# Building the expert gate table in two halves of 64 tiles instead of one table of 128

## The chip, the cores and the metric

One core of one Trainium2 chip runs the whole program in one launch. The metric is the device time of one execution in microseconds (us), median over runs.

## The reference

A two-layer decoder trunk over 256 tokens with a model width of 1024. Layer 0 mixes by a short gated convolution, layer 1 by attention; behind each stands the same expert mixer, and only that one is touched here. For each token it picks, per head, 16 of 128 x 128 experts, and sums gate x gelu(x . u) x v over them:

```python
q = (xc @ w_q).reshape(PEER_CHUNK, PEER_HEADS, 2, PEER_HALF)
s1 = einsum('thd,nd->thn', q[:, :, 0], sub_k1); s2 = einsum('thd,nd->thn', q[:, :, 1], sub_k2)
v1, i1 = top_k(s1, 16); v2, i2 = top_k(s2, 16)
cand = v1[..., :, None] + v2[..., None, :]
cidx = i1[..., :, None] * 128 + i2[..., None, :]
top_s, top_pos = top_k(cand, 16)
e_idx = take_along_axis(cidx, top_pos); g = softmax(top_s)
a = gelu(einsum('td,thkd->thk', xc, u_emb[e_idx]))
out = einsum('thk,thkd->td', g * a, v_emb[e_idx])
```

## The kernel before, in words

The kernel computes the mixer densely. All 16384 experts are gone through as 128 **tiles** of 128 experts; a tile is one item of a list that every stage takes its weights from (`items`, line 93). `A` holds, for 128 experts (partitions), 128 tiles and 256 tokens, first gelu(x . u), and after multiplication by the gate table the weight of each expert for each token. An expert's number is 128 x e1 + e2, where e1 is the tile and e2 the partition.

**Getting an item ready.** Weights arrive by DMA into one of three `RAW` buffers (`issue`, line 126). A u tile is turned by VectorE into `TR` (line 153). ScalarE rounds the item to a reduced 4-byte format as `HI` (line 164), and the difference goes into `LO` (line 168): on GpSimd, in two pieces of 128x512, for u tiles; on VectorE, in one piece of 128x1024, for v tiles. Each kind of buffer exists three times. `next_item` (line 213) prepares items n+1 to n+3, issues the products of item n and then lets `run_side` issue side work.

**u tiles** (`u_mm`, line 885). 24 products of 128x256: 16 with HI (lines 748, 749) and 8 with LO (line 752), into one half of a PSUM bank of the lower four (`lo4`). After each odd tile `out_pair` applies Gelu to the pair.

**v tiles** (line 988). 12 products of 128x512 (line 453), with `A` as the stationary operand, accumulate the output in the upper four banks (`hi4`). Every four tiles `wsplit` (lines 962, 963) splits the next four slices of `A` on ScalarE and VectorE.

**Side work.** A queue of operations with a price each; every item brings a budget (1.62 for u tiles, 1.25 for v tiles), and an operation is issued when the budget covers it. During the first u tiles this is the top-k search. After it, `listed` (line 831) turns the lists of e1, e2 and gate to the tokens, and `g_side` (line 895) builds the gate table, 8 tokens at a time, 32 groups per layer:

- `hots` (line 909): one VectorE comparison of 128x2048 makes the one-hot rows of e1 and e2 for 8 tokens;
- `gated` (line 918), twice: a VectorE product of 128x1024 puts the gate, in two parts, into the one-hot of e1, for 4 tokens each;
- its matmuls (line 925): 8 for each `gated`, 128 x 128 stationary, 128 columns moving, into `hi4`; issued on TensorE after a later u tile's products;
- `copied` (line 935): for tiles whose Gelu is still to come, ScalarE copies the table into `A`;
- `mult` (line 942): for tiles whose Gelu is done, VectorE multiplies `A` by the table.

A pair whose Gelu comes when part of the table already lies in `A` is multiplied by it afterwards, in `out_pair` (lines 864, 868 and 872). All of the table is built beside the u tiles: `u_last` empties the side queue before the first v tile.

Of the kernel before, what the change touches and what calls it, by code (L numbers as in the profile page):

```python
# [35 lines left out]
def trunk_kernel(ctx: ExitStack, tc, x, norm_mix, norm_ffn, conv_w_in, conv_w, conv_w_out,  # L36
# [26 lines left out]
    iota_t = sb.tile([128, 128, 2], F16, name="iota_t")  # L63
    OH = xbuf.bitcast(F16).rearrange("p (a b k t) -> p a b k t", a=5, b=TOK // 2, t=2)
    OH2 = (OH[:, 0], OH[:, 2])
    OH1 = OH[:, 1]
    ohg2 = sb.tile([128, 2, TOK // 4, 128, 2], F16, name="ohg2")
    OHG = [OH[:, 3 + i].rearrange("p (a b) k t -> p a b k t", a=2) for i in range(2)] + [ohg2]
    eT = sb.tile([128, T // TOK, 2, TOK // 2, 2], F16, name="eT")
    gT2 = sb.tile([128, T // 4, 2, 2, 2], F16, name="gT2")  # L70
# [211 lines left out]
    def late_consts():  # L282
        cwr = scratch(16384, 128)
        sp.dma_start(cwr[0:24], conv_w[0].rearrange("k (c p) -> (k c) p", p=128))
        pool.iota(iota_t, pattern=[[1, 128], [0, 2]], base=0, channel_multiplier=0,
                  allow_small_or_imprecise_dtypes=True)
# [407 lines left out]
    def peer(l):  # L694
# [27 lines left out]
        U0 = Q0 + H  # L722
        on_pool.update(range(Q0, U0))
# [119 lines left out]
        gates = lists[2].rearrange("p (s b t) -> p s b t", b=2, t=2)
# [5 lines left out]
        st = {"tiles": 0, "toks": 0, "prod": deque(), "multed": 0, "copied": deque(), "late": None, "listed": False}  # L849

        def late():

            f, st["late"] = st["late"], None
            if f:
                f()

        def out_pair(j, bk):

            late()
            assert 2 * j + 2 <= 95 or st["listed"]  # L860
            k, n = 2 * j, st["toks"]
            v = bk.rearrange("p (k t) -> p k t", t=256)
            if n:
                act.activation(v[:, :, 0:n], v[:, :, 0:n], AF.Gelu)

                def f():
                    w = A[:, k:k + 2, 0:n]
                    dve.scalar_tensor_tensor(w, v[:, :, 0:n], 1.0 / GSC, w, op0=OP.mult, op1=OP.mult)  # L868
                st["late"] = f
                credit[0] -= 0.1 + 0.0021 * n  # L870
            if n < T:
                act.activation(A[:, k:k + 2, n:T], v[:, :, n:T], AF.Gelu)  # L872
            st["tiles"] = k + 2

        def prod(before=NI, last=2 * T):

            while st["prod"]:
                n, q, f = st["prod"][0]
                if n > before or q > last or q // 2 > st["multed"] + 1:
                    return  # L880
                st["prod"].popleft()
                f()
                credit[0] += 0.45

        def u_mm(k):
            def f(hi, lo):
# [3 lines left out]
                if k % 2:  # L890
                    out_pair(k // 2, bk)
# [3 lines left out]
        def g_side():  # L895

            NG = T // TOK

            def tk(s, k0, k1):
                return psum[:, 2048 + s % 2 * 1024:3072 + s % 2 * 1024].rearrange(  # L900
                    "p (t k) -> p k t", k=128)[:, k0:k1]

            def spread(v):

                return v.rearrange("p a b t -> p (a b) t")[:, :, None, :].to_broadcast([128, TOK, 128, 2])

            def hots(s):
                a = s % 2
                dve.tensor_tensor(OH[:, a:a + 2].rearrange("p a b k t -> p (a b) k t"),  # L909
                                  iota_t[:, None].to_broadcast([128, TOK, 128, 2]), spread(eT[:, s]), op=OP.is_equal)  # L910

            def gated(q):

                s, h = q // 2, q % 2
                prod(last=q - 3)
                assert len(st["prod"]) < 3
                g = OHG[q % 3]
                dve.tensor_tensor(g, OH1[:, None, 2 * h:2 * h + 2].to_broadcast([128, 2, 2, 128, 2]),  # L918
                                  gT2[:, q, :, :, None, :].to_broadcast([128, 2, 2, 128, 2]), op=OP.mult)
# [7 lines left out]
                st["prod"].append((state["use"], q, f))  # L927

            def copied(s):

                prod(last=2 * s + 1)
                assert not st["prod"] or st["prod"][0][1] > 2 * s + 1
                n, t = st["tiles"], slice(s * TOK, s * TOK + TOK)
                if n < NK:
                    act.activation(A[:, n:NK, t], tk(s, n, NK), AF.Copy)
                st["copied"].append(n)
                st["toks"] += TOK
# [49 lines left out]

        for k in range(NK - 3):
            m = k // 4
            if k % 4 == 1 and m + 1 < NK // 4:  # L990
                wsplit(m + 1)
# [10 lines left out]
            next_item(mm_tok(*v_args(k)), 1.25)  # L1002
# [78 lines left out]
```

## Time and profile before

| what | value |
|---|---|
| median of 3 runs | 1941.55 us (1938.91 to 1941.59) |
| the profiled execution, its own time | 1941.85 us |
| its span | 1939.8 us |
| TensorE matmul busy | 1823.6 us (94%), 12095 instructions |
| VectorE busy | 1399.5 us (72%), 2023 instructions |
| ScalarE busy | 894.2 us (46%) |
| GpSimd busy | 866.4 us (45%) |
| mean HBM traffic | 166 GB/s |

The span is what the profiler saw between the first and the last instruction; the execution's own time has 2.05 us around it. Shares over the whole span are means over stages that differ, so what follows is read by stage. In layer 0 the u tiles start at 147.7 us and the v tiles at 603.4 us; in layer 1 they start at 1126.6 and 1582.9 us. In the rows, PE is the matmul side of TensorE and PEld its weight load, DVE is VectorE, ACT ScalarE, POOL GpSimd.

### The profile page before, as it was taken

What the parts mean: (1) busy time and instruction counts of PE and PEld (TensorE: products, weight loads), DVE (VectorE), ACT (ScalarE), POOL (GpSimd) and SP (SyncE); (2) the same over time, 40 slices, a digit from 0 to 9 for tenths busy, and PEclk for the clock granted to TensorE, in tenths of its full rate; (3) what the DMA queues carried; (4) which work ended last, traced back from release to release, by engine and by line L of the source; (5) the groups of instructions that cost most, each with busy time, mean ns of one, the idle gap of its engine ahead of it and who ended that gap; (6) DMA issues with size and microseconds to landing.
All of it is one profiled execution on the core that took longest, in us unless ns stands there. A gap on an engine that the chain in (4) does not pass through costs nothing.

```text
span 1939.8 us, 32552 instructions
## 1 busy us (share of the span) xinstructions
PE 1823.6 (94%) x12095; PEld 1660.7 (86%) x12095; DVE 1399.5 (72%) x2023; ACT 894.2 (46%) x1149; POOL 866.4 (45%) x573
## 2 busy tenths in 40 slices
PE   7999999898779999999999999999988799999998
PEld 7989999898779888888788799999988798888886
DVE  4758798999986555555554488889999965555555
ACT  4345544443335454544445544554433344544443
POOL 2248799887761000000163588898877620000000
PEclk9999999999999999999899999999999899999999
DMA  6566555444445655655452466564444355556664
GB/s 196 163 176 197 162 173 162 128 136 130 131 123 172 195 195 193 223 195 193 143 174 86 145 196 176 153 184 122 139 127 136 101 179 192 194 194 227 194 192 136
DMA packets 217267, 321.67 MB, mean 166 GB/s; under 512 B 26236, under 2 KB 174228, under 8 KB 216596
## 3 DMA queue, kind: packets, MB, share of 16 engines
q1 hardware_dynamic: 214836, 313.11, 53.4%
q10 hardware_dynamic: 2272, 6.49, 0.9%
q8 instruction: 94, 1.54, 0.3%
q14 instruction: 65, 0.53, 0.1%
HBM read 316.35 MB, written 3.15 MB: 165 GB/s over the span
## 4 chain that ended last, share of the span: by engine, by line
PE 67%; DVE 16%; issue 6%; DMA 6%; POOL 3%; ACT 1%; SPq 1%; DVEq 0%; ACTq 0%; POOLq 0%
PE psum L453 38%; PE psum L748 7%; PE psum L749 7%; PE psum L752 7%; DMA raw<-in_peer_u_dram 5%; DVE tr L153 5%; DVE xbuf L918 4%; POOL lo L168 3%; PE psum L440 3%; DVE ohg L918 2%; DVE xbuf L909 2%; DVE big L942 1%; SPq L133 1%; DVE big L868 1%; PE psum L462 1%
## 5 line engine op out<-in xcount | busy, mean ns | idle before, releaser
L168 POOL TENSOR_TENSOR lo<-tr,hi 128x512 fp32r<-128x512 f32 x496 | 733.6, 1512 | 159.2 <-ACT hi L164 145.6
L168 DVE TENSOR_TENSOR lo<-raw,hi 128x1024 fp32r<-128x1024 f32 x286 | 351.7, 1231 | 347.9 <-ACT hi L164 347.3
L164 ACT ACTIVATE hi<-raw 128x1024 fp32r<-128x1024 f32 x336 | 355.6, 1060 | 428.2 <-PE psum L453 340.7
L748 PE MATMUL psum<-xh,hi 128*128 128x256 f32 x2160 | 550.4, 291 | 0.0
L749 PE MATMUL psum<-xl,hi 128*128 128x256 f32 x2160 | 541.3, 287 | 0.3
L453 PE MATMUL psum<-hi,xh 128*128 128x512 f32 x1112 | 431.7, 390 | 0.0
L453 PE MATMUL psum<-hi,xl 128*128 128x512 f32 x1112 | 430.7, 389 | 0.0
L749 PEld LDWEIGHTS psum<-xl,hi 128*128 128x128 f32 x2160 | 423.9, 196 | 1.1 <-DVE xl L356 0.9
L748 PEld LDWEIGHTS psum<-xh,hi 128*128 128x128 f32 x2160 | 423.6, 196 | 0.7 <-ACT xh L351 0.5
L164 ACT ACTIVATE hi<-tr 128x1024 fp32r<-128x1024 f32 x256 | 270.4, 1058 | 290.4 <-DVE tr L153 256.0
L168 POOL TENSOR_TENSOR lo<-raw,hi 128x1024 fp32r<-128x1024 f32 x50 | 121.4, 2442 | 534.1 <-ACT hi L164 528.0
L153 DVE STREAM_TRANSPOSE tr<-raw 128x1024 f32<-128x1024 f32 x256 | 315.5, 1233 | 51.2 <-POOL lo L168 30.1
L752 PE MATMUL psum<-xh,lo 128*128 128x256 f32 x2160 | 308.7, 285 | 7.9 <-POOL lo L168 7.7
L453 PE MATMUL psum<-lo,xh 128*128 128x512 f32 x1112 | 297.3, 389 | 0.0
L752 PEld LDWEIGHTS psum<-xh,lo 128*128 128x128 f32 x2160 | 281.3, 193 | 11.5 <-POOL lo L168 11.1
L453 PEld LDWEIGHTS psum<-lo,xh 128*128 128x128 f32 x1112 | 208.7, 188 | 43.4
L453 PEld LDWEIGHTS psum<-hi,xl 128*128 128x128 f32 x1112 | 208.8, 188 | 43.3
L453 PEld LDWEIGHTS psum<-hi,xh 128*128 128x128 f32 x1112 | 208.5, 188 | 42.9
L1025 POOL TENSOR_TENSOR big<-xbuf,big 128x256 f32<-128x256 f32 x2 | 1.4, 738 | 363.3 <-DVE rstd L321 363.3
L925 PEld LDWEIGHTS <-xbuf 128*128 128x128 f16 x1024 | 65.6, 100 | 74.1 <-issue 70.8
L918 DVE TENSOR_TENSOR xbuf<-xbuf,gT 128x1024 f16<-128x1024 f16 x86 | 126.9, 1491 | 0.9
L872 ACT ACTIVATE big<-psum 128x512 f32<-128x512 f32 (+14 forms) x116 | 57.2, 493 | 101.6 <-PE psum L752 99.8
(156 smaller groups left out, 1495.6 us busy)
## 6 DMA issues: line engine op xcount, KB each, us to landing
raw<-in_peer_u_dram SPq DMA_DIRECT2D x1024, 128.0 KB, 2.9
raw<-in_peer_v_dram SPq DMA_DIRECT2D x256, 512.0 KB, 4.3
raw<-in_conv_w_in_dram SPq DMA_DIRECT2D x96, 128.0 KB, 2.7
raw<-in_attn_w_qkv_dram SPq DMA_DIRECT2D x96, 128.0 KB, 2.5
raw<-in_peer_w_q_dram SPq DMA_DIRECT2D x64, 128.0 KB, 2.7
raw<-in_conv_w_out_dram SPq DMA_DIRECT2D x8, 512.0 KB, 3.8
raw<-in_attn_w_o_dram SPq DMA_DIRECT2D x8, 512.0 KB, 3.7
x_dram<-xbuf ACTq DMA_DIRECT2D x2, 1024.0 KB, 4.1
```

The lines of the kernel that those rows point to most:

```text
L153: dve.transpose(TR[m % 3].rearrange("p b (g i) -> p g b i", g=4), RAW[m % 3].rearrange("p (g m) -> p g m", m=256))
L164: act.activation(HI[m % 3], src, AF.Copy)
L168: eng.tensor_sub(LO[m % 3][:, c], src[:, c], HI[m % 3][:, c])
L440: pe.matmul(banks[c // 2][:, (c % 2) * 256:(c % 2) * 256 + 256], w[:, c * 128:c * 128 + 128], xx[:, b], start=(b == 0 and p == 0 and c % 2 ...
L453: pe.matmul(banks[j], x[:, j // 2 * 128:j // 2 * 128 + 128], w[:, j % 2 * 512:j % 2 * 512 + 512], start=(first and p == 0), stop=(last and ...
L748: pe.matmul(o, hi[:, s], XH[:, b], start=(b == 0), stop=False)
L749: pe.matmul(o, hi[:, s], XL[:, b], start=False, stop=False)
L752: pe.matmul(o, lo[:, s], XH[:, b], start=False, stop=(b == 7))
L872: act.activation(A[:, k:k + 2, n:T], v[:, :, n:T], AF.Gelu)
L909: dve.tensor_tensor(OH[:, a:a + 2].rearrange("p a b k t -> p (a b) k t"), iota_t[:, None].to_broadcast([128, TOK, 128, 2]), spread(eT[:, s ...
L918: dve.tensor_tensor(g, OH1[:, None, 2 * h:2 * h + 2].to_broadcast([128, 2, 2, 128, 2]), gT2[:, q, :, :, None, :].to_broadcast([128, 2, 2, ...
L925: pe.matmul(o, OH2[s % 2][:, 2 * h + t // 2, :, t % 2], g[:, a, t // 2, :, t % 2], start=(a == 0), stop=(a == 1))
```

## The change

The gate table is built in two halves of 64 tiles. The first half (tiles 0 to 63) may be started when u tile 63 is done, so that every tile it needs has its Gelu; it runs beside the last 64 u tiles, into `hi4`. The second half (tiles 64 to 127) starts with the first v tile and runs beside v tiles, into `lo4`; `wsplit` for tile 64 needs it, and it is emptied before that. Each half has 32 groups of 8 tokens. A group is one comparison of 128x1536 (three blocks of 64: for the first half e1, e2, e2 - 64; for the second e2, e2 - 64, e1 - 64), one product of 128x1024, 16 matmuls with 64 columns moving, and one `mult` of 128x512 (64 tiles x 8 tokens). `copied` and the later multiplication in `out_pair` are gone: Gelu is one ScalarE operation per pair. `listed` makes six lists of 128x256 in place of four of 128x128. The v tiles' budget is 1.7 in place of 1.25. Lines of the changed kernel: comparison 876, product 884, matmuls 891, `mult` 898, turn 152, LO 167, v products 452, `wsplit` 918 and 919.

```diff
-            for a in range(2):
-                for m in range(2):
-                    v = lists[1 - (a + m) % 2].rearrange("p (s m b t) -> p s m b t", m=2, b=TOK // 2, t=2)
-                    act.activation(eT.rearrange("p (s m) a b t -> p s m a b t", m=2)[:, :, m, a], v[:, :, m], AF.Copy)
+            e1, e2 = (v.rearrange("p (s b t) -> p s b t", b=TOK // 2, t=2) for v in lists[0:2])
+            for hf, rows in enumerate((((e1, 0.0), (e2, 0.0), (e2, -64.0)), ((e2, 0.0), (e2, -64.0), (e1, -64.0)))):
+                for r, (e, less) in enumerate(rows):
+                    act.activation(eT[hf][:, :, :, r], e, AF.Copy, bias=less)
...
                 if k % 2:
-                    out_pair(k // 2, bk)
+                    assert k < 95 or st["listed"]
+                    act.activation(A[:, k - 1:k + 1].rearrange("p k t -> p (k t)"), bk, AF.Gelu)
                 prod(state["use"] - 1)
...
+            def hots(s):
+                prod(last=s - 2)
+                dve.tensor_tensor(HOT[s % 2].rearrange("p b (r k) t -> p b r k t", r=3),
+                                  iota_t[:, None, None].to_broadcast([128, TOK // 2, 3, 64, 2]),
+                                  eT[hf][:, s, :, :, None, :].to_broadcast([128, TOK // 2, 3, 64, 2]),
+                                  op=OP.is_equal)
+
+            def gated(s):
+                one_hot = HOT[s % 2][:, :, 128 * hf:128 * hf + 64]
+                pairs = HOT[s % 2][:, :, 64 - 64 * hf:192 - 64 * hf]
+                dve.tensor_tensor(OHG[s % 2], one_hot[:, None].to_broadcast([128, 2, TOK // 2, 64, 2]),
+                                  gT2[:, s, :, :, None, :].to_broadcast([128, 2, TOK // 2, 64, 2]), op=OP.mult)
 
                 def f():
-                    for t in range(4):
-                        o = hi4[s % 2 * 2 + h][:, t * 128:t * 128 + 128]
+                    for t in range(TOK):
+                        o = banks[s % 4][:, t * 64:t * 64 + 64]
                         for a in range(2):
-                            pe.matmul(o, OH2[s % 2][:, 2 * h + t // 2, :, t % 2], g[:, a, t // 2, :, t % 2],
+                            pe.matmul(o, pairs[:, t // 2, :, t % 2], OHG[s % 2][:, a, t // 2, :, t % 2],
                                       start=(a == 0), stop=(a == 1))
...
             def mult(s):
-                n, t = st["copied"].popleft(), slice(s * TOK, s * TOK + TOK)
-                w = A[:, 0:n, t]
-                dve.scalar_tensor_tensor(w, tk(s, 0, n), 1.0 / GSC, w, op0=OP.mult, op1=OP.mult)
-                st["multed"] += 1
+                prod(last=s)
+                w = A[:, half, s * TOK:s * TOK + TOK]
+                dve.scalar_tensor_tensor(w, banks[s % 4].rearrange("p (t k) -> p k t", k=64), 1.0 / GSC, w,
+                                         op0=OP.mult, op1=OP.mult)
 
             for s in range(NG + 3):
                 if s >= 3:
-                    add(0.9, mult, s - 3)
-                if 2 <= s < NG + 2:
-                    add(0.0, copied, s - 2)
+                    add(0.95, mult, s - 3, gate=gate)
                 if s < NG:
-                    add(1.25, hots, s)
-                    add(0.7, gated, 2 * s)
-                    add(0.7, gated, 2 * s + 1)
+                    add(1.45, hots, s, gate=gate)
+                    add(1.2, gated, s, gate=gate)
 
         add(0.0, st.update, listed=True)
-        g_side()
+        g_side(0, hi4, U0 + 64)
+        before = len(side)
+        g_side(1, lo4, V0)
+        second = len(side) - before
```

VectorE beside the gated u tiles, before: L153 turns a u tile, L909 is the comparison, L918 the products, L942 `mult`, L868 the later multiplication of a pair.

```order
L909 TENSOR_TENSOR xbuf<-iota_t,eT 128x2048
L918 TENSOR_TENSOR xbuf<-xbuf,gT_86 128x1024 x2
L153 STREAM_TRANSPOSE tr_70<-raw_67 128x4x8x32
L942 SCALAR_TENSOR_TENSOR big<-psum,big 128x88x8
L909 TENSOR_TENSOR xbuf<-iota_t,eT 128x2048
L153 STREAM_TRANSPOSE tr_71<-raw_68 128x4x8x32
L868 SCALAR_TENSOR_TENSOR big<-psum,big 128x2x136
```

The same place now (L152 turns, L876 compares, L884 is the product, L898 `mult`):

```order
L876 TENSOR_TENSOR xbuf<-iota_t,eT_84 128x1536
L884 TENSOR_TENSOR xbuf<-xbuf,gT_86 128x1024
L152 STREAM_TRANSPOSE tr_71<-raw_68 128x4x8x32
L898 SCALAR_TENSOR_TENSOR big<-psum,big 128x64x8
L152 STREAM_TRANSPOSE tr_69<-raw_66 128x4x8x32
```

A group has one product where it had two, a smaller comparison, a `mult` of fixed size, and no L868.

VectorE beside the v tiles, where only LO and `wsplit` stood, now (L167 is LO, L919 `wsplit`):

```order
L876 TENSOR_TENSOR xbuf<-iota_t,eT_85 128x1536
L919 TENSOR_TENSOR xl<-big,xh 128x1024
L167 TENSOR_TENSOR lo_77<-raw_68,hi_74 128x1024
L884 TENSOR_TENSOR xbuf<-xbuf,gT_86 128x1024
L898 SCALAR_TENSOR_TENSOR big<-psum,big 128x64x8
L167 TENSOR_TENSOR lo_75<-raw_66,hi_72 128x1024
```

The second half's operations stand between the LOs of the first 50 or so v tiles.

TensorE beside those v tiles now, at the end of a v tile; before, the next v tile's first product followed the LO products at once:

```order
L452 MATMUL psum<-lo_77,xh 128x512 x4
L891 LDWEIGHTS xbuf
L891 MATMUL psum<-xbuf 128x64
L891 LDWEIGHTS xbuf
```

Such a run has 16 pairs of load and matmul, and there are 32 runs among the v tiles of a layer, 32 more among its u tiles (before: 32 of the u tiles' 128-column kind in all).

## Rows read from the trace of the kernel before

**Rows 1.** Busy time of each engine in stretches of layer 0

```profile
core 0: us, PE busy (x) PEld busy (x) DVE busy (x) ACT busy (x) POOL busy (x), PEclk, DMA share, GB/s
200.00:250.00 50.00, 50.00 (x419) 49.98 (x418) 42.90 (x147) 25.44 (x29) 42.26 (x34) 1.00 0.63 175
346.80:473.60 126.80, 113.92 (x1060) 112.32 (x1058) 126.49 (x120) 52.73 (x82) 104.59 (x65) 0.97 0.46 134
473.60:580.40 106.80, 85.69 (x757) 84.40 (x755) 101.91 (x86) 37.40 (x60) 74.39 (x50) 0.95 0.44 127
603.40:940.00 336.60, 336.60 (x1488) 278.73 (x1487) 188.91 (x157) 164.08 (x160) 0.00 (x0) 1.00 0.61 199
```

**Rows 2.** Line 749 alone (8 matmuls per u tile), both layers

```profile
195.80:242.00 46.20, 30.57 (x125) 24.04 (x126) 1.00 0.58 161
320.20:603.40 283.20, 142.52 (x568) 111.70 (x568) 0.97 0.47 134
346.80:473.60 126.80, 64.03 (x256) 50.12 (x256) 0.97 0.46 134
580.40:603.40 23.00, 13.74 (x56) 10.75 (x56) 1.00 0.48 146
1297.90:1582.90 285.00, 144.00 (x568) 113.03 (x568) 0.96 0.46 134
```

**Rows 3.** VectorE's groups by line, 346.8 to 580.4 us

```profile
line engine op names shapes xcount | busy us, mean ns | idle before us <-releasers
L153 DVE STREAM_TRANSPOSE tr<-raw 128x1024 f32<-128x1024 f32 x58 | 71.2, 1228 | 3.4 <-POOL lo L168 1.8 <-ACT psum L864 1.6
L918 DVE TENSOR_TENSOR xbuf<-xbuf,gT 128x1024 f16<-128x1024 f16 x39 | 57.1, 1479 | 0.4
L909 DVE TENSOR_TENSOR xbuf<-iota_t,eT 128x2048 f16<-128x2048 f16 x29 | 45.8, 1579 | 0.0
L918 DVE TENSOR_TENSOR ohg<-xbuf,gT 128x1024 f16<-128x1024 f16 x19 | 29.2, 1539 | 0.2
```

**Rows 4.** Lines 909 and 918 over the span: duration ns min/median/max

```profile
L909 DVE TENSOR_TENSOR xbuf<-iota_t,eT x64: 1175/1440/2348, 327.7 to 1537.8; 128x2048 f16<-128x2048 f16 x64
L918 DVE TENSOR_TENSOR xbuf<-xbuf,gT x86: 641/1676/1787, 329.7 to 1541.6; 128x1024 f16<-128x1024 f16 x86
```

**Rows 5.** GpSimd's line 168: alone (147.7 to 200 us), then from 346.8 to 580.4 us

```profile
L168 POOL TENSOR_TENSOR lo<-tr,hi x35: 1279/1302/1317, 146.6 to 199.3; 128x512 fp32r<-128x512 f32 x35
...
L168 POOL TENSOR_TENSOR lo<-tr,hi 128x512 fp32r<-128x512 f32 x115 | 181.4, 1606 | 54.6 <-ACT hi L164 53.7 <-ACT psum L864 0.5
```

**Rows 6.** `mult` of 128x512, VectorE by form, 346.8 to 580.4 us

```profile
L942 DVE SCALAR_TENSOR_TENSOR big<-psum,big 128x512 f32<-128x512 f32 x1 | 0.7, 669 | 0.0
```

**Rows 7.** Weight loads around a group of 16 table matmuls: start us, us, instructions

```profile
373.07 0.92 PEld L925 LDWEIGHTS <-xbuf 128*128 128x128 f16 x16
373.95 0.19 PEld L748 LDWEIGHTS psum<-xh,hi 128*128 128x128 f32 x1
```

**Rows 8.** Attention's 4-byte matmuls, 128 and 64 columns: start us, us

```profile
1052.35 0.27 PE L645 MATMUL psum<-ident,big 128*128 128x128 f32 x1
1052.46 0.38 PE L647 MATMUL psum<-ident,big 128*128 128x128 f32 x2
1052.68 0.33 PE L658 MATMUL psum<-big 128*128 128x64 f32 x2
1052.85 0.39 PE L659 MATMUL psum<-big 128*128 128x64 f32 x2
1053.07 0.39 PE L660 MATMUL psum<-big 128*128 128x64 f32 x2
1053.30 0.28 PE L658 MATMUL psum<-big 128*128 128x64 f32 x1
```

**Rows 9.** Load durations ns min/median/max, lines 925 and 659

```profile
L925 PEld LDWEIGHTS <-xbuf x1024: 96/97/149, 335.4 to 1547.5; 128*128 128x128 f16 x171
L659 PEld LDWEIGHTS psum<-big x32: 192/192/192, 1052.8 to 1066.0; 128*128 128x128 f32 x32
```

**Rows 10.** VectorE's groups beside the v tiles, 603.4 to 940 us

```profile
L168 DVE TENSOR_TENSOR lo<-raw,hi 128x1024 fp32r<-128x1024 f32 x124 | 152.0, 1226 | 147.4 <-ACT hi L164 147.3
L963 DVE TENSOR_TENSOR xl<-big,xh 128x1024 fp32r<-128x1024 f32 x32 | 39.0, 1219 | 0.6 <-ACT xh L962 0.6
```

**Rows 11.** ScalarE's list copies, by form, 300 to 346 us

```profile
L840 ACT ACTIVATE eT<-psum 128x128 f16<-128x128 f32 x4 | 0.8, 283 | 0.9 <-PE psum L835 0.9
L841 ACT ACTIVATE gT<-psum 128x256 f16<-128x256 f32 x1 | 0.4, 415 | 0.0
```

More of the change, by code (lines that the diff above doesn't have):

```diff
@@ L62, in trunk_kernel @@
     XT = [xo[:, i * D:i * D + D] for i in range(2)]
[L63 to L70, printed above, removed]
+    iota_t = sb.tile([128, 64, 2], F16, name="iota_t")
+    xh16 = xbuf.bitcast(F16)
+    HOT = [xh16[:, i * 2560:i * 2560 + 1536].rearrange("p (b k t) -> p b k t", b=TOK // 2, t=2) for i in range(2)]
+    OHG = [xh16[:, i * 2560 + 1536:i * 2560 + 2560].rearrange("p (a b k t) -> p a b k t", a=2, b=TOK // 2, t=2)
+           for i in range(2)]
+    eT = [sb.tile([128, T // TOK, TOK // 2, 3, 2], F16, name=f"eT{i}") for i in range(2)]
+    gT2 = sb.tile([128, T // TOK, 2, TOK // 2, 2], F16, name="gT2")
     ident = sb.tile([128, 128], F32, name="ident")
@@ L284, in late_consts @@
         sp.dma_start(cwr[0:24], conv_w[0].rearrange("k (c p) -> (k c) p", p=128))
-        pool.iota(iota_t, pattern=[[1, 128], [0, 2]], base=0, channel_multiplier=0,
+        pool.iota(iota_t, pattern=[[1, 64], [0, 2]], base=0, channel_multiplier=0,
                   allow_small_or_imprecise_dtypes=True)
@@ L722, in peer @@
         U0 = Q0 + H
+        V0 = U0 + NK
         on_pool.update(range(Q0, U0))
@@ L836, in listed @@
                 pe.transpose(lists[2][:, t], gg[:, i].rearrange("p h n -> p (h n)"), ident)
-            for a in range(2):
-                for m in range(2):
-                    v = lists[1 - (a + m) % 2].rearrange("p (s m b t) -> p s m b t", m=2, b=TOK // 2, t=2)
-                    act.activation(eT.rearrange("p (s m) a b t -> p s m a b t", m=2)[:, :, m, a], v[:, :, m], AF.Copy)
+            e1, e2 = (v.rearrange("p (s b t) -> p s b t", b=TOK // 2, t=2) for v in lists[0:2])
+            for hf, rows in enumerate((((e1, 0.0), (e2, 0.0), (e2, -64.0)), ((e2, 0.0), (e2, -64.0), (e1, -64.0)))):
+                for r, (e, less) in enumerate(rows):
+                    act.activation(eT[hf][:, :, :, r], e, AF.Copy, bias=less)
             act.activation(gT2[:, :, 0], gates, AF.Copy, scale=GSC)
-        gates = lists[2].rearrange("p (s b t) -> p s b t", b=2, t=2)
+        gates = lists[2].rearrange("p (s b t) -> p s b t", b=TOK // 2, t=2)
         pause(2)
@@ L847, in peer, with prod @@
         add(0.4, dve.scalar_tensor_tensor, gT2[:, :, 1], gates, GSC, gT2[:, :, 0], op0=OP.mult, op1=OP.subtract)
[L849 to L883, printed above, removed]
+        asked = deque()
+        st = {"listed": False}
+        def prod(before=NI, last=T):
+            while asked and asked[0][0] <= before and asked[0][1] <= last:
+                asked.popleft()[2]()
+                credit[0] += 0.6
         def u_mm(k):
@@ L890, in f, with g_side @@
                 if k % 2:
-                    out_pair(k // 2, bk)
+                    assert k < 95 or st["listed"]
+                    act.activation(A[:, k - 1:k + 1].rearrange("p k t -> p (k t)"), bk, AF.Gelu)
                 prod(state["use"] - 1)
             return f
-        def g_side():
+        def g_side(hf, banks, gate):
             NG = T // TOK
[L899 to L905, printed above, removed]
-            def hots(s):
[L908 to L919, printed above, removed]
@@ new lines, in g_side @@
+            half = slice(64 * hf, 64 * hf + 64)
+            def hots(s):
+                prod(last=s - 2)
[8 more added lines that the diff above has]
+                                  gT2[:, s, :, :, None, :].to_broadcast([128, 2, TOK // 2, 64, 2]), op=OP.mult)
@@ L926, in f @@
                                       start=(a == 0), stop=(a == 1))
[L927 to L937, printed above, removed]
+                asked.append((state["use"], s, f))
@@ L967, in u_last @@
             bk = lo4[(NK // 2 - 1) % 4]
-            drain_side()
-            late()
             for b in range(8):
@@ L975, in u_last @@
                 if b == 3:
+                    drain_side(second)
                     wsplit(0)
-            out_pair(NK // 2 - 1, bk)
-            late()
+            act.activation(A[:, NK - 2:NK].rearrange("p k t -> p (k t)"), bk, AF.Gelu)
         for k in range(NK - 1):
@@ L986, in v_args, with v_mm, f @@
             return hi4, WH[m % 2][:, k % 4], WL[m % 2][:, k % 4], k == 0, k == NK - 1
+        def v_mm(k):
+            mm = mm_tok(*v_args(k))
+            def f(hi, lo):
+                mm(hi, lo)
+                prod(state["use"] - 1)
+            return f
         for k in range(NK - 3):
@@ L990, in peer @@
             if k % 4 == 1 and m + 1 < NK // 4:
+                if m == 15:
+                    drain_side()
                 wsplit(m + 1)
@@ L1001, in peer @@
                     act.activation(GN, GN, AF.Copy, scale=-0.5)
-            next_item(mm_tok(*v_args(k)), 1.25)
+            next_item(v_mm(k), 1.7)
         y = scratch(3 * D, 2 * D)
```

## The prediction

> **What bounds the kernel now.** I read the busy times by stretch first, then the pace of the tiles, then the groups of the engine that is full. Over the span TensorE looks like the bound, but not where the change is. While the gate table is built beside the u tiles of layer 0 (346.8 to 580.4 us), VectorE is busy 126.49 of 126.80 us in the first part and 101.91 of 106.80 in the second, while TensorE and GpSimd have gaps [rows 1]. Beside the v tiles it is the other way: TensorE is busy all 336.60 us, VectorE 188.91, GpSimd not at all. The pace says the same. Line 749 runs 8 times in a tile: 16 tiles without a table take 46.2 us, 2.89 each, which is also that of the last tiles (8 in 23.0 us); 32 tiles with it take 126.8 us, 3.96 each [rows 2]. A v tile takes 336.6 / 124 = 2.71 us. So each u tile with table work loses about 1.1 us, and the v tiles have VectorE time free.
>
> What fills VectorE is seen in its groups: per tile a turn of 1.23 us, and per group of 8 tokens a comparison of 1.58 and two products of 1.48 to 1.54 us on the mean [rows 3]. These two kinds are slow there only: at best the comparison takes 1.175 and the product 0.641 us, at the median 1.44 and 1.676 [rows 4]. GpSimd's 128x512 piece takes 1.30 us before the table starts and 1.61 beside it [rows 5]. Table operations of VectorE and LO pieces of GpSimd lengthen each other. By the Trainium skill (SBUF — State Buffer, section "SBUF: two separate sides") VectorE operations with two operands in SBUF and GpSimd operations hold one shared port in turn, each for its whole length. By that rule the two add up on one port, and the sum below would be 3.4 us or more per tile; without it, it would be TensorE's 3.25.
>
> **The change, part by part**, for each layer from u tile 56 to the first v tile, now 283.2 us in layer 0 and 285.0 in layer 1 [rows 2].
>
> *Tiles 56 to 63.* The table starts at about tile 58 now and only after tile 64 with the change, so these 8 run near the bare pace; some top-k work may still be there: 8 x 3.0 = 24.0 us.
>
> *The first half*, 32 groups beside some 58 tiles (65 to 122 by the order), 0.55 a tile. New durations: the comparison of 1536 in place of 2048 elements, 0.75 x 1.175 = 0.88 us; one product, 0.64; a `mult` of 0.67 [rows 6]. The pace is the largest of three:
> - *VectorE*: a turn of 1.23, and 0.55 x (0.88 + 0.64 + 0.67) = 1.20 without waits: 2.43. With the mean waits of now (1.58 - 1.175 = 0.40 for a comparison, 1.50 - 0.64 = 0.86 for a product) 3.13; if each waits as long as a product at the median does (1.03), 3.56.
> - *The lengthening with GpSimd*, taken as a full sum: two LO pieces, 2.60, and 0.55 x (0.88 + 0.64) = 0.84: 3.44. I try this sum on now: 29 comparisons and 58 products in 56 tiles [rows 3, 4] are 0.52 x 1.175 + 1.04 x 0.64 = 1.27, with 2.60 it is 3.87, where 3.96 was measured, 2% over.
> - *TensorE*: 2.89 + 0.55 of a group's matmuls. Before, 16 weight loads go from 373.07 to the next tile's first load at 373.95: 0.88 us, 0.055 a pair, and with the slower change to the tile's own matmuls about 0.96 [rows 7]. With 64 columns in place of 128 a pair lies between half of that (0.44 + 0.08 = 0.52 a group) and the same 0.96. For 4-byte operands the pairs stand 0.11 us apart at 128 columns and at 64 alike [rows 8]: there the weight load sets the spacing. But the f16 load's record is 97 ns against 192 [rows 9], 95 less, so it may set no more than 0.11 - 0.095 = 0.015 us a pair, and the columns decide. I take 0.65, nearer the low end: 2.89 + 0.36 = 3.25.
>
> The sum with GpSimd is largest; with the 2% it is 3.5, and I take that. Its ends are 3.18 (TensorE alone, with 0.52) and the 3.96 of now. The 6 last tiles need 2.88 each, 17.3 us. So 24.0 + 58 x 3.5 + 17.3 = 244.3 us, **38.9 less in layer 0, 40.7 in layer 1**.
>
> *The second half* beside the v tiles: 32 groups of matmuls that were not there, and TensorE is full, so all of it lies on the path: 32 x 0.65 = **20.8 us more per layer** (16.6 to 30.7). VectorE: LO 1.23 and a quarter of 1.22 for `wsplit` [rows 10], and over some 50 v tiles 0.64 x 2.19 = 1.40: 2.94 a tile, against TensorE's 2.71 + 0.64 x 0.65 = 3.13. It fits, with 6% to spare: GpSimd is idle there, so no operation is lengthened. Queued behind a comparison are LO and `wsplit`; TensorE, which would wait for LO, has three LO buffers and reads LO in the last third of a tile. If that cover goes, the second half costs what VectorE takes beyond TensorE.
>
> *The rest* I put at nothing. The copies and the second multiplications that go were on ScalarE, half idle, and on VectorE (they are in the old pace). Six list copies of 0.415 us in place of four of 0.283 [rows 11] add 1.4 us once per layer to ScalarE, hidden by the items made ready ahead; without that cover 1.4 us each. No weight load from HBM is moved on its queue, and GpSimd's queue keeps its order. The buffer of the one-hots is now in use up to about v tile 55, and is loaded anew at v tile 72. The granted clock is 0.95 to 0.97 in the gated stretch and 1.00 outside [rows 1]; VectorE decides there, so I give it no term.
>
> The sum: -(38.9 + 40.7) + 2 x 20.8 = -38.0 us on the profiled execution's 1941.85: **1904 us**. The median of the runs, 1941.55, is 0.3 lower, less than a measurement tells apart here (0.2%, 3.9 us).
>
> **The rivals.**
> - *A: GpSimd and VectorE do not add up, TensorE becomes the bound of the first half, and halved columns halve the matmul.* Pace 2.89 + 0.55 x 0.52 = 3.18: 24.0 + 184.4 + 17.3 = 225.7, 57.5 + 59.3 us less, and 2 x 16.6 back: 1858 us. For it: GpSimd still idles 54.6 of 233.6 us, waiting for VectorE's turns [rows 5]. Against: the sum with GpSimd explains the pace of now within 2%. 0.17.
> - *B: a table pair costs 0.055 us whatever its columns.* Then the v tiles get 2 x 30.7 us and the first half, with TensorE at 2.89 + 0.53 = 3.42, stays at 3.5: 1941.85 - 79.6 + 61.4 = 1924 us. For it: the 4-byte rows, where halving the columns gave nothing. Against: the shorter f16 load. 0.18.
> - *C, slower: the first half keeps the pace of 3.96.* Fewer table operations on VectorE let its turns come earlier, so GpSimd's idle time fills with LO work, and each table operation finds it busy and waits the full 1.03 us, each turn then waits for GpSimd's release of `TR`, and the saved product is lost in waits. Then 24.0 + 229.7 + 17.3 = 271.0: only 12.2 + 14.0 us less against 41.6 more: 1957 us. It decides from a pace of 3.83 on, where gain and price are equal. For it: at the full wait VectorE alone already needs 3.56. Against: a product fewer per group is 1.5 us of VectorE's time, and turns waited for GpSimd only 1.8 us in 233.6 [rows 3]. 0.13.
> - *D: an f16 weight load sets the spacing as the 4-byte one does, 0.112 us.* A group is 1.79 us; pace 3.87, 266.0 us, 17.2 + 19.0 less, and 114.6 more: 2020 us. Against it speaks that 16 f16 pairs already go at 0.055. 0.02. The Trainium skill (TensorE: Matmul & The Clock Gate, section "LDWEIGHTS (loading the stationary operand)") puts a load at its columns / 1.2 in ns whatever the type, 107 ns here, an estimate by which the time would be about 2012 us. The 4-byte rows agree with it, the f16 rows do not.
> - *No change to be measured*, gain and price equal by chance: 0.02.
>
> **How the numbers follow.** The forecast, 1904, has 0.48; its own range is 1885 to 1918 (pace 3.35 to 3.6). A, B, C, D and no change have 0.17, 0.18, 0.13, 0.02 and 0.02. Faster by over 0.2% are the forecast, A and B: 0.83. Slower are D and most of C: 0.13. The same: the rest of C and no change, 0.04. The range 1860 to 1945 leaves out D, the upper two thirds of C (0.09) and the lower half of A (0.08).
>
> **What would show it.** In the changed profile: u tiles 64 to 120 at about 3.5 us each, with VectorE no longer full and GpSimd near full; the product at most as long as now there, and at 0.64 us beside v tiles, the comparison at 0.88; 32 groups among about 50 v tiles of a layer, each 0.5 to 0.7 us of TensorE, with v tiles between them at 2.71; LO never waited for there. Wrong would make it: a pace of 3.2 or less or over 3.8; pairs at 0.055 us or more; TensorE waiting for LO or for the products among the v tiles.

## The result, and the profile after

The changed kernel takes 1860.01 us (median of 4 runs, 1859.85 to 1860.8) against 1941.57 us before: 0.958 of it, 95% interval 0.9564 to 0.9597. The profiled execution's span goes from 1939.8 to 1858.8 us. I had forecast 38 us; it is 81.6.

Where it came from, by the stretches of [rows 2]: line 749 alone (8 matmuls per u tile) and, in the second view, the v products' line 452 (12 per v tile) in the changed kernel.

```profile
core 0: us, PE busy (x) PEld busy (x), PEclk, DMA share, GB/s
318.30:544.50 226.20, 139.27 (x568) 109.04 (x568) 1.00 0.56 169
342.00:520.30 178.30, 109.85 (x448) 86.01 (x448) 1.00 0.55 165
1256.70:1482.90 226.20, 139.28 (x568) 109.04 (x568) 1.00 0.57 169
```

```profile
544.50:900.60 356.10, 345.32 (x1487) 276.87 (x1488) 1.00 0.58 188
1482.90:1839.00 356.10, 345.29 (x1487) 276.87 (x1488) 1.00 0.58 188
```

The same two counts in the kernel before, line 749 over the 56 tiles from 64 to 119 and line 453 over 124 v tiles:

```profile
346.80:580.40 233.60, 113.10 (x448) 88.69 (x448) 0.96 0.45 130
```

```profile
603.40:940.40 337.00, 336.88 (x1487) 279.06 (x1488) 1.00 0.61 198
1582.90:1919.90 337.00, 336.88 (x1487) 279.15 (x1488) 1.00 0.62 198
```

From u tile 56 to the first v tile a layer now takes 226.2 us, 57.0 and 58.8 less than before. The 56 tiles from 64 to 119 take 178.3 / 56 = 3.18 us each, where they took 233.6 / 56 = 4.17 before: the first 32 of them 3.96, the last 24 of them 106.8 / 24 = 4.45 [rows 1]. 124 v tiles take 356.1 us where they took 337.0, 2.72 a tile: 19.1 us more per layer. That makes -115.8 + 38.2 = -77.6 us. Of the other 3.4 us of the span 1.9 lie before tile 56 of layer 0, 1.4 between v tile 124 of layer 0 and u tile 56 of layer 1, and 0.1 at the end.

Every engine while the first half of the table is built (tiles 64 to 95, then 96 to 119) and beside the v tiles of the changed kernel:

```profile
core 0: us, PE busy (x) PEld busy (x) DVE busy (x) ACT busy (x) POOL busy (x), PEclk, DMA share, GB/s
342.00:443.80 101.80, 101.80 (x1042) 101.07 (x1041) 80.22 (x84) 41.96 (x49) 101.80 (x65) 1.00 0.55 165
443.80:520.30 76.50, 76.50 (x791) 75.94 (x787) 60.36 (x64) 31.30 (x37) 76.50 (x49) 1.00 0.56 167
544.50:707.00 162.50, 162.50 (x1107) 131.85 (x1107) 142.74 (x157) 72.80 (x72) 0.00 (x0) 1.00 0.53 175
```

In the first half VectorE, full before [rows 1], is down to 79%; TensorE *and* GpSimd are busy all the time. Beside the v tiles that build the second half TensorE is full and VectorE at 88%. The granted clock is 1.00, where it was 0.97 and 0.95 in the gated stretch with TensorE's gaps.

VectorE's groups in the same first half, GpSimd's pieces (ns min/median/max), and what waits there:

```profile
L152 DVE STREAM_TRANSPOSE tr<-raw 128x1024 f32<-128x1024 f32 x57 | 70.7, 1241 | 33.6 <-POOL lo L167 33.6
L876 DVE TENSOR_TENSOR xbuf<-iota_t,eT 128x1536 f16<-128x1536 f16 x30 | 31.6, 1053 | 5.0 <-PE psum L891 5.0
L884 DVE TENSOR_TENSOR xbuf<-xbuf,gT 128x1024 f16<-128x1024 f16 x31 | 27.3, 879 | 0.2
L898 DVE SCALAR_TENSOR_TENSOR big<-psum,big 128x512 f32<-128x512 f32 x29 | 19.5, 671 | 0.0
```

```profile
L884 DVE TENSOR_TENSOR xbuf<-xbuf,gT x31: 641/650/1678, 342.7 to 517.8; 128x1024 f16<-128x1024 f16 x31
...
L167 POOL TENSOR_TENSOR lo<-tr,hi x113: 1282/1752/2083, 341.4 to 519.5; 128x512 fp32r<-128x512 f32 x113
```

The product had a median of 1.676 us in [rows 4]; here it is 0.650, its bare time, though GpSimd is busier than before. GpSimd's pieces are lengthened as before (a median of 1.75 us, on the mean 1.63 against 1.61 [rows 5], where a piece alone takes 1.30), and VectorE's turns wait 33.6 us for GpSimd, not 1.8 [rows 3]. In order of time on VectorE, then three of GpSimd's pieces in the same stretch:

```profile
405.22 1.25 DVE L152 STREAM_TRANSPOSE tr<-raw 128x1024 f32<-128x1024 f32 x1 [1.19 <-POOL lo L167]
406.39 0.65 DVE L884 TENSOR_TENSOR xbuf<-xbuf,gT 128x1024 f16<-128x1024 f16 x1
406.96 0.68 DVE L898 SCALAR_TENSOR_TENSOR big<-psum,big 128x512 f32<-128x512 f32 x1
408.23 1.25 DVE L152 STREAM_TRANSPOSE tr<-raw 128x1024 f32<-128x1024 f32 x1 [0.59 <-POOL lo L167]
409.40 0.92 DVE L876 TENSOR_TENSOR xbuf<-iota_t,eT 128x1536 f16<-128x1536 f16 x1
```

```profile
406.40 1.79 POOL L167 TENSOR_TENSOR lo<-tr,hi 128x512 fp32r<-128x512 f32 x1
...
408.16 1.30 POOL L167 TENSOR_TENSOR lo<-tr,hi 128x512 fp32r<-128x512 f32 x1
...
409.41 2.06 POOL L167 TENSOR_TENSOR lo<-tr,hi 128x512 fp32r<-128x512 f32 x1
```

A turn starts when GpSimd ends a tile and lasts 1.25 us, about one GpSimd piece (1.30). The one table operation (comparison or product) behind it therefore comes as GpSimd changes pieces: the product at 406.39 and the comparison at 409.40 us, each 0.01 us ahead of a piece. That piece is the longer one, 1.79 us behind the product and 2.06 behind the comparison; the piece beside the turn keeps its 1.30.

TensorE's side: the weight loads of one group beside v tiles, and the next tile's first two products.

```profile
601.62 0.54 PEld L891 LDWEIGHTS <-xbuf 128*128 128x128 f16 x16 [0.26 <-issue]
602.10 0.19 PEld L452 LDWEIGHTS psum<-hi,xh 128*128 128x128 f32 x1
```

```profile
602.12 0.48 PE L452 MATMUL psum<-hi,xh 128*128 128x512 f32 x1
602.43 0.40 PE L452 MATMUL psum<-hi,xl 128*128 128x512 f32 x1
```

16 pairs take 602.10 - 601.62 = 0.48 us, 0.030 a pair, against 0.055 in [rows 7]: fewer columns did make the pairs shorter. A group costs 19.1 / 32 = 0.60 us, about 0.1 more than its pairs. Most of that is the change to the next tile's products, the first two of which start 0.31 us apart where a v tile's twelve products otherwise start 2.72 / 12 = 0.23 apart.

### The profile page after: what moved, and what is told of

The parts are those of the page before. It is cut to its first block, busy times and chain, and to the rows that moved or that the text cites. A ratio compares the mean times of both kernels' runs of the same rounds, so it can differ in the third digit from the quotient of the medians.

```text
span 1858.8 us, 34504 instructions
## 1 busy us (share of the span) xinstructions
PE 1811.7 (97%) x13119; PEld 1639.3 (88%) x13119; DVE 1329.0 (71%) x2083; ACT 859.9 (46%) x1033; POOL 860.7 (46%) x573
## 3 DMA queue, kind: packets, MB, share of 16 engines
q8 instruction: 102, 1.67, 0.4%
## 4 chain that ended last, share of the span: by engine, by line
PE 92%; POOL 2%; DVE 2%; issue 1%; ACT 1%; DMA 1%; SPq 0%; ACTq 0%; POOLq 0%; DVEq 0%
PE psum L452 41%; PE psum L748 13%; PE psum L752 13%; PE psum L749 13%; PE psum L891 3%; PE psum L439 3%; POOL lo L167 2%; PE psum L461 1%; PE psum L460 1%; PE psum L459 1%; PE psum L763 1%; DVE big L498 1%; DMA big<-in_x_dram 0%; DVE big L496 0%; PE psum L589 0%
## 5 line engine op out<-in xcount | busy, mean ns | idle before, releaser
L167 POOL TENSOR_TENSOR lo<-tr,hi 128x512 fp32r<-128x512 f32 x496 | 727.8, 1505 | 47.6 <-ACT hi L163 37.8
L748 PE MATMUL psum<-xh,hi 128*128 128x256 f32 x2160 | 539.1, 287 | 0.0
L749 PE MATMUL psum<-xl,hi 128*128 128x256 f32 x2160 | 532.0, 284 | 0.3
L167 DVE TENSOR_TENSOR lo<-raw,hi 128x1024 fp32r<-128x1024 f32 x286 | 351.1, 1229 | 239.5 <-ACT hi L163 234.1
L452 PE MATMUL psum<-hi,xh 128*128 128x512 f32 x1112 | 437.5, 395 | 0.0
L749 PEld LDWEIGHTS psum<-xl,hi 128*128 128x128 f32 x2160 | 416.1, 193 | 1.1 <-DVE xl L355 0.9
L748 PEld LDWEIGHTS psum<-xh,hi 128*128 128x128 f32 x2160 | 415.7, 192 | 0.7 <-ACT xh L350 0.5
L152 DVE STREAM_TRANSPOSE tr<-raw 128x1024 f32<-128x1024 f32 x256 | 317.3, 1239 | 125.7 <-POOL lo L167 111.6
L167 POOL TENSOR_TENSOR lo<-raw,hi 128x1024 fp32r<-128x1024 f32 x50 | 122.2, 2458 | 552.9 <-ACT hi L163 542.7
L865 ACT ACTIVATE big<-psum 128x512 f32<-128x512 f32 x126 | 75.2, 597 | 301.7 <-PE psum L752 301.7
L876 DVE TENSOR_TENSOR xbuf<-iota_t,eT 128x1536 f16<-128x1536 f16 x128 | 128.8, 1006 | 23.9 <-PE psum L891 23.9
L884 DVE TENSOR_TENSOR xbuf<-xbuf,gT 128x1024 f16<-128x1024 f16 x128 | 99.7, 779 | 1.1
```

The source lines that it names most:

```text
L152: dve.transpose(TR[m % 3].rearrange("p b (g i) -> p g b i", g=4), RAW[m % 3].rearrange("p (g m) -> p g m", m=256))
L167: eng.tensor_sub(LO[m % 3][:, c], src[:, c], HI[m % 3][:, c])
L452: pe.matmul(banks[j], x[:, j // 2 * 128:j // 2 * 128 + 128], w[:, j % 2 * 512:j % 2 * 512 + 512], start=(first and p == 0), stop=(last and ...
L748: pe.matmul(o, hi[:, s], XH[:, b], start=(b == 0), stop=False)
L749: pe.matmul(o, hi[:, s], XL[:, b], start=False, stop=False)
L865: act.activation(A[:, k - 1:k + 1].rearrange("p k t -> p (k t)"), bk, AF.Gelu)
```

## The experiments

Two pairs of theories. On the pace: **P**, TensorE alone sets the 3.18 us; **G**, GpSimd, lengthened by the table operations, is at its limit as well. On the lengthening: **L**, table operations and GpSimd's pieces exclude each other, so that a table operation right behind another one sits out a whole piece; **S**, they share bandwidth and slow each other in proportion. A ratio is to the kernel before, run beside the variant. The two variants with half the matmuls were run once each and have no ratio; what is read from them are paces, which both layers give alike.

**Half of the first half's table matmuls**

```diff
-                        for a in range(2):
+                        for a in range(1 if hf == 0 else 2):
...
-                                      start=(a == 0), stop=(a == 1))
+                                      start=(a == 0), stop=(hf == 0 or a == 1))
```

The first half leaves out the gate's second, small part.

> The first half issues 8 of its 16 table matmuls per group (the gate's second, small part is left out there; everything else stays). Measured so far: u tiles 64 to 120 at 3.18 us each, TensorE and GpSimd both busy all the time. Theory P (TensorE alone sets the first half's pace): a group falls from 0.57 to about 0.33 us, the pace to 2.88 + 0.55 x 0.33 = 3.06, GpSimd gets idle time or not but TensorE waits for nothing, total about 1846 us. Theory G (GpSimd, lengthened by VectorE's table operations, is at its limit as well): two pieces of 1.26 us and 0.55 x (0.49 + 0.76) for the table operations make 3.15 to 3.2; the pace stays at 3.13 or more, TensorE now waits for LO, total 1855 to 1860 us.

Measured 1855.34 us. The first half by engine, whole and in its first 32 and last 24 tiles, and two of its waits:

```profile
342.50:518.10 175.60, 174.89 (x1587) 170.79 (x1586) 139.01 (x144) 73.41 (x85) 175.60 (x111) 1.00 0.56 166
...
342.50:441.60 99.10, 98.83 (x907) 97.25 (x906) 78.80 (x81) 41.87 (x49) 99.10 (x63) 1.00 0.55 165
441.60:518.10 76.50, 76.06 (x687) 73.54 (x684) 60.21 (x64) 31.54 (x37) 76.50 (x49) 1.00 0.57 167
```

```profile
DVE tr L152 <- POOL lo L167: 33.7, 39, 1.2
...
PEld psum L752 <- POOL lo L167: 1.9, 6, 0.3
```

The pace falls only to 175.6 / 56 = 3.14, in layer 1 too; GpSimd is still never idle, and TensorE begins to wait for LO, 1.9 us in all. That is G. The 3.14 is a mean: 99.1 / 32 = 3.10 in the first 32 tiles, 76.5 / 24 = 3.19 in the last 24, which is what they took with all matmuls.

**Every fourth LO of the last u tiles on VectorE**

```diff
+        on_dve.update(range(U0 + 68, V0 - 4, 4))
```

> LO of every fourth of the last u tiles moves from GpSimd to VectorE, nothing is left out. P and G both: TensorE's demand of 3.18 stays, so 1860 us within 3; GpSimd gets a quarter of its time free, VectorE goes from about 79% to about 89%. If the pace falls below 3.16, neither holds. If VectorE's longer queue delays its turns, the pace rises to 3.25 or more (1868 us and up).

Measured 1861.16 us, 0.959 of before (0.9574 to 0.9606): no change against the changed kernel's 0.958. GpSimd is free for 48.9 of 178.30 us, and the pace is the same 3.18:

```profile
344.80:523.10 178.30, 178.30 (x1827) 177.01 (x1826) 163.12 (x161) 73.67 (x85) 129.40 (x86) 1.00 0.57 165
```

**Both at once**

> Half of the first half's table matmuls left out, as in the run with 8 matmuls per group, and every fourth LO on VectorE. P: the same as with the matmuls alone. G: only here does the pace fall to about 3.06 (total about 1846 us), since GpSimd's limit is out of the way. If it stays at 3.13 or more here too, the limit is neither TensorE nor GpSimd.

Measured 1847.09 us. The 56 tiles now take 171.10 us, 3.055 each, in both layers, with TensorE full again:

```profile
343.20:514.30 171.10, 171.10 (x1587) 169.81 (x1586) 167.84 (x157) 74.58 (x85) 132.56 (x85) 1.00 0.58 168
```

So two limits lie 0.05 us apart in the changed kernel: TensorE at 3.18 us per tile, GpSimd at 3.14 on the mean. Only the removal of both brings the pace that P gave for the first alone.

**Three comparisons of one block**

```diff
-                dve.tensor_tensor(HOT[s % 2].rearrange("p b (r k) t -> p b r k t", r=3),
...
+                for r0, r1 in ((0, 1), (1, 2), (2, 3)):
+                    dve.tensor_tensor(HOT[s % 2].rearrange("p b (r k) t -> p b r k t", r=3)[:, :, r0:r1],
...
```

> The comparison of three blocks becomes three comparisons of one block (128x512 each), one behind the other; same elements, same results. Theory L (VectorE's table operations and GpSimd's pieces take turns on something exclusive, so that a table operation right behind another one first sits out a whole GpSimd piece): the second and third comparison take about 1.3 us each instead of 0.35, VectorE needs 2.5 + 0.55 x 2.2 = 3.7 us per u tile in the first half, total about 1860 + 2 x 58 x 0.5 = 1915 us; beside v tiles, where GpSimd is idle, no lengthening beyond the fixed cost of two more operations. Rival S (they share bandwidth, each is slowed by the other's load in proportion): three comparisons take about 0.2 us more in all, inside VectorE's spare time, total 1860 to 1865 us.

Measured 1908.25 us, 0.984 of before (0.9824 to 0.9857). Every engine in the first half, VectorE's comparison there, then the comparison beside v tiles:

```profile
340.60:537.90 197.30, 185.62 (x1825) 182.60 (x1824) 197.30 (x201) 72.59 (x83) 155.82 (x111) 0.97 0.49 144
```

```profile
L877 DVE TENSOR_TENSOR xbuf<-iota_t,eT 128x512 f16<-128x512 f16 x88 | 95.2, 1132 | 0.0
```

```profile
L877 DVE TENSOR_TENSOR xbuf<-iota_t,eT x92: 416/420/428, 569.8 to 729.7; 128x512 f16<-128x512 f16 x92
```

The same operation takes 0.42 us where GpSimd is idle and 1.13 on the mean beside it. VectorE is full again (197.30 of 197.30 us), the pace is 3.52, the v tiles take the same 356.2 us. S gave 5 us at most; 48 were measured. So with three operations in place of one for the three blocks the change would have kept only about 33 of its 81.6 us; all of the loss is beside u tiles.

**LO of a u tile in one piece**

```diff
-            for h in range(2 if is_u(m) and eng is pool else 1):
-                c = slice(512 * h, 512 * h + 512) if is_u(m) and eng is pool else slice(0, 1024)
-                eng.tensor_sub(LO[m % 3][:, c], src[:, c], HI[m % 3][:, c])
+            eng.tensor_sub(LO[m % 3], src, HI[m % 3])
```

> GpSimd makes LO of a u tile in one piece of 128x1024 (2.44 us measured for that size) instead of two of 1.30 each. Theory L (exclusive turns): a turn is released when a piece ends and takes 1.24 us, so the table operation behind it comes in the middle of a long piece and waits some 1.2 us: the product's median goes from 0.65 to about 1.8 us in the first half, the comparison's from 0.92 to about 2.1; VectorE and GpSimd then alternate at 3.1 to 3.3 us per tile, total 1860 to 1875 us. Rival S (shared bandwidth): one piece less fixed cost, the product stays under 1.0 us, total 1855 to 1861 us.

Measured 1885.66 us, 0.9711 of before (0.9694 to 0.9727).

```profile
L882 DVE TENSOR_TENSOR xbuf<-xbuf,gT x30: 1723/1748/2820, 349.6 to 528.5; 128x1024 f16<-128x1024 f16 x30
```

The product's median is the 1.8 us of L, its shortest 1.72. The comparison's median, 1.40, came out shorter than the 2.1 expected. The pace is 3.27, inside the expectation; the time is 10 us over it, since the u tiles before the table lose 7 us per layer too. Neither theory spoke of that, and its cause is not shown.

**Each table matmul as two of 32 columns**

```diff
-                            pe.matmul(o, pairs[:, t // 2, :, t % 2], OHG[s % 2][:, a, t // 2, :, t % 2],
-                                      start=(a == 0), stop=(a == 1))
+                        for c in (0, 32):
+                            for a in range(2):
+                                pe.matmul(o[:, c:c + 32], pairs[:, t // 2, :, t % 2],
+                                          OHG[s % 2][:, a, t // 2, c:c + 32, t % 2],
+                                          start=(a == 0), stop=(a == 1))
```

> Each table matmul of 64 columns becomes two of 32, each with its own weight load: twice the pairs, the same columns. If columns set a pair's spacing (0.031 us at 64 columns, 0.0575 at 128: 0.0267 per 64 columns and 0.004 fixed), a pair takes 0.0175 and a group 0.64 instead of 0.57 us: 2 x 64 x 0.07 = 9 us more, about 1869 us. If 0.03 us is a floor of weight load or issue, a group takes 32 x 0.031 + 0.08 = 1.07 us: beside v tiles 2 x 32 x 0.5 = 32 us more, in the first half a pace of 2.88 + 0.55 x 1.07 = 3.47, 34 us more: about 1926 us.

Measured 1903.05 us, 0.9806 of before (0.9789 to 0.9822), between the two. The loads of one group:

```profile
604.37 0.87 PEld L892 LDWEIGHTS <-xbuf 128*128 128x128 f16 x32 [0.26 <-issue]
605.17 0.19 PEld L452 LDWEIGHTS psum<-hi,xh 128*128 128x128 f32 x1
```

(605.17 - 604.37) / 32 = 0.025 us a pair. From 128 to 64 columns the spacing goes from 0.055 to 0.030, from 64 to 32 only to 0.025.

**`mult` ahead of the product, first half**

```diff
+            def both(s):
+                if s >= 3:
+                    mult(s - 3)
+                if s < NG:
+                    gated(s)
...
+                if hf == 0:
+                    if s < NG:
+                        add(1.8, hots, s, gate=gate)
+                    add(1.8 if s < NG else 0.95, both, s, gate=gate)
+                    continue
```

> In the first half mult of an earlier group stands ahead of the product, so that the product comes 1.9 us behind a turn's start and not 1.24. Theory L with timing (a turn lasts about as long as a GpSimd piece, so what follows it finds the port at a change of pieces): the product now comes inside the second piece and waits about 0.7 us, its median goes from 0.65 to about 1.3 us; the pace stays near 3.18 or goes to 3.25, total 1860 to 1870 us. Rival (the wait depends only on how busy GpSimd is): the product keeps its mean of 0.88 and median of 0.65, total 1860 us.

Measured 1860.0 us, 0.9579 of before (0.9563 to 0.9595).

```profile
L884 DVE TENSOR_TENSOR xbuf<-xbuf,gT x30: 648/1307/1709, 345.8 to 517.8; 128x1024 f16<-128x1024 f16 x30
```

The product's median doubles to 1.307 us, as L with timing gave, with no operation added or changed in size, only the order of issue. The time does not move: VectorE has room for it.

**The product as two of 128x512**

```diff
-                dve.tensor_tensor(OHG[s % 2], one_hot[:, None].to_broadcast([128, 2, TOK // 2, 64, 2]),
-                                  gT2[:, s, :, :, None, :].to_broadcast([128, 2, TOK // 2, 64, 2]), op=OP.mult)
+                for a in range(2):
+                    dve.tensor_tensor(OHG[s % 2][:, a], one_hot,
+                                      gT2[:, s, a, :, None, :].to_broadcast([128, TOK // 2, 64, 2]), op=OP.mult)
```

> The product of 128x1024 becomes two of 128x512, one behind the other (as the kernel before had two per group). Theory L: the first takes about 0.38 us, the second sits out a GpSimd piece, about 1.3 to 1.4 us; VectorE needs 2.5 + 0.55 x 1.1 = 3.1 us per u tile of the first half, at the edge of the pace of 3.18: total 1860 to 1880 us. Rival S: both about 0.4 us, total 1860 us.

Measured 1871.17 us, 0.9635 of before (0.9619 to 0.9651).

```profile
L885 DVE TENSOR_TENSOR xbuf<-xbuf,gT x60: 375/1444/1523, 343.3 to 521.7; 128x512 f16<-128x512 f16 x60
```

0.375 us at best, 1.444 at the median. In order of time the second of the two takes 1.48 to 1.52 us in every one of the 30 groups: it sits out a piece. The first takes 0.38 in 22 of them. The pace is 3.25.

**The kernel before, its table operations spaced**

```diff
+            def spaced(s):
+                gated(2 * s)
+                if s >= 3:
+                    mult(s - 3)
+                gated(2 * s + 1)
+
...
-                if s >= 3:
+                if s >= NG:
                     add(0.9, mult, s - 3)
...
-                    add(1.25, hots, s)
-                    add(0.7, gated, 2 * s)
-                    add(0.7, gated, 2 * s + 1)
+                    add(1.75, hots, s)
+                    add(1.8, spaced, s)
```

> The kernel before, with nothing changed but the order of VectorE's table operations beside u tiles: mult stands between the two products of a group, and the comparison mostly stands apart from them. Table operations right behind another table operation fall from 46 per layer to 12; no operation is added, removed or made larger or smaller. Theory L: some 33 waits of a GpSimd piece (about 1.0 us each) go per layer, shorter waits behind mult (0.3 us) come in their place: some 25 us per layer at most, total 1895 to 1920 us; the mean of the products falls from 1.49 to about 1.1. Rival S: 1941 us within 5, products as long as before.

Measured 1928.99 us, 0.994 of before (0.9924 to 0.9957): 12 us, where 21 was the least that was expected. Every engine in tiles 64 to 95 and 96 to 119, the products of that stretch (343.7 to 575.1 us) and the waits from 346.8 to 570 us:

```profile
343.70:482.60 138.90, 118.83 (x1062) 117.12 (x1059) 118.78 (x121) 52.32 (x83) 105.25 (x67) 0.94 0.43 126
482.60:575.10 92.50, 83.53 (x769) 82.23 (x769) 83.26 (x85) 35.56 (x59) 74.48 (x48) 0.99 0.45 129
```

```profile
L918 DVE TENSOR_TENSOR xbuf<-xbuf,gT x39: 641/1239/1748, 348.2 to 564.5; 128x1024 f16<-128x1024 f16 x39
L918 DVE TENSOR_TENSOR ohg<-xbuf,gT x20: 641/970/1714, 343.5 to 562.1; 128x1024 f16<-128x1024 f16 x20
```

```profile
PE psum L925 <- DVE big L942: 29.0, 25, 3.3
DVE xbuf L918 <- PE psum L925: 20.8, 20, 3.2
DVE ohg L918 <- PE psum L925: 7.2, 9, 1.1
```

The kernel before, from 346.8 to 580.4 us:

```profile
PE psum L925 <- DVE big L942: 34.0, 20, 5.3
```

The lengthening goes as L has it: medians of 1.24 and 0.97 us in place of 1.67. But a new wait takes its place: the products now wait 28 us for TensorE's table matmuls, while those wait 29 us for `mult` to free their two pairs of banks. VectorE is no longer full, and the pace over the 56 tiles is still 231.4 / 56 = 4.13, against 4.17 before: the first 32 tiles lose (4.34 against 3.96), the last 24 gain (3.85 against 4.45). Table matmuls waited 34.0 us for `mult` in the kernel before too, but there VectorE never waited for them. The edit sets each `mult` behind the next comparison and one product, so this wait may be in part of its own making; that it was a second limit of the kernel before is not shown. In the changed kernel, where a group takes one bank of four, TensorE waits for no `mult` in the first half, and VectorE waits 5.0 us for the matmuls.

## Why the prediction was wrong

The sign was right, the size was not: 1904 us forecast, 1860.01 measured, at the very end of the range, and rival A's 1858 us is nearest to it.

- *The bound before* was VectorE, as read.
- *The step that failed: "The sum with GpSimd is largest; with the 2% it is 3.5, and I take that."* The pace is 3.18. Over 58 tiles that is 18.6 us per layer, 37 of the 43.6 us that are missing. Two things were wrong in it.
  - First, the sum was sized too high: 3.44 by the rows, where GpSimd's limit is 3.14 (half the matmuls, GpSimd busy 175.60 of 175.60 us). Undisturbed pieces start 1.26 us apart, not 1.30 (the median before the table starts; 408.16 to 409.41 above is such a pair). And a table operation does not cost GpSimd its whole length: 0.49 us for the product of 0.65 (a piece of 1.79 in place of 1.30), 0.76 for the comparison of 0.92 (2.06). With 30 groups in 56 tiles that makes 2 x 1.26 + 0.54 x (0.49 + 0.76), about 3.2, as the last 24 tiles showed with half the matmuls.
  - Second, the 2% by which the old pace stood over the old sum looked like a proof of it. It was none, because the two belong to different stretches: the operations were counted over 56 tiles, 3.96 is the pace of the first 32. Those 56 tiles take 4.17, 8% over the sum of 3.87. The last 24 take 4.45, where their 11 comparisons and 22 products give 3.73. GpSimd also stood idle for 54.6 of these 233.6 us [rows 5], so its sum did not set the old pace; VectorE did, full or nearly so [rows 1], with operations that sat out pieces. That the sum met the first 32 tiles was chance.
- *Rival A's time came out near, its reason only in part.* It had GpSimd and VectorE not adding up, and TensorE as the bound. They do add up in part: two pieces alone are 2.60 us a tile, GpSimd's limit beside the table is 3.14, just under TensorE's 3.18. TensorE's own sum holds: 30 groups in 56 tiles at the 0.60 us measured beside v tiles, on 2.88, make 3.20, and the 8 pairs that the run with both leaves out, at 0.030 us each, are the 0.13 us by which its pace falls. That A's total lies within 2 us is partly luck: its price beside the v tiles is 5 us too low, and 3.4 us came off outside its terms.
- *VectorE*, put between 2.43 and 3.56, needs about 79% of 3.18, near 2.5: its waits shrank to about 0.2 us a tile (on the mean 1.05 us for a comparison and 0.88 for a product, where 0.92 and 0.64 are the shortest). I had carried over the mean waits of before, or more; they belong to the old order, with two or three table operations in a row. With one behind each turn there is mostly none. Rival C named the very wait that now orders it, turns that wait for GpSimd's release of `TR` (33.6 us), and drew the wrong end from it: the wait makes each table operation come at a change of pieces.
- *A table group on TensorE* was 0.65 in the sum and cost 0.60 beside v tiles: 19.1 us per layer against 20.8, 3 of the missing 43.6 us. At 64 columns the pairs stand 0.030 us apart, not 0.055 or 0.112: B and D fell. (The 2012 us given beside D come to 2010 by D's own terms.)
- *Beside the v tiles* TensorE was full and never waited for LO, as put. Comparison and product took 0.95 and 0.69 us there, a little over the 0.88 and 0.64 put. What I had put at nothing came to 3.4 us less, whose cause is not shown.
- *The first tiles*: 8 x 3.0 was near, (342.0 - 318.3) / 8 = 2.96.

The Trainium skill's rule on the shared port (SBUF — State Buffer, section "SBUF: two separate sides"), that whichever starts first keeps it for the whole instruction and the other blocks, agrees with VectorE's side of these runs: the second of two products takes 1.5 us where 0.375 is its bare time, 1.1 us more, most of a piece. On GpSimd's side a piece lost 0.49 us to a product of 0.65, less than the whole. What failed was the pace that I drew from the rule by adding full lengths.

## What to carry to other kernels

Where operations of two engines exclude each other, count the operations that stand back to back and not their elements alone: three operations in place of one cost 48 us here. An operation of about the other engine's length that the other does not lengthen, placed ahead of each, takes the waits away: here a turn of 1.25 us, beside pieces of 1.30. And a sum that meets the old time within 2% is no proof of its mechanism: take its counts and the time from the same stretch, test it on a second stretch, and ask whether the engine it names was busy all that time.

## What the runs showed of the hardware

- An f16 matmul with its own 128-column weight load stands 0.055 us after the one before at 128 columns, 0.030 at 64 and 0.025 at 32: the second halving saves only 0.005. The Trainium skill (TensorE: Matmul & The Clock Gate, section "Back-to-back issue gap") gives, for an isolated matmul, an issue floor of about 25 ns at 1 to 64 columns. The pairs with 32 columns stand at that figure; at 64 the spacing is still above it.
- The change from table matmuls to the tile's own products costs about 0.1 us a group (0.60 per group against 0.48 for its 16 pairs), a price of the number of groups.
- Beside GpSimd's pieces a comparison or product of VectorE that starts while a piece runs is lengthened by up to most of a piece (0.42 us to 1.13 on the mean for a comparison of 128x512). The turn (1.22 to 1.25 us over the whole span) and `mult` (0.67 us beside pieces, 0.68 beside v tiles) are not.
